# Every fourth half of the latents' weights gets its low part from a ScalarE negative and an adding GpSimd transfer

## The chip, the cores and the metric

The kernel runs on one core of a Trainium2 chip. The metric is the device time of one execution in microseconds, the median of several runs. Before the change it is 989.68 us (three runs, 989.65 to 989.76).

## The reference

One layer of a generator over 256 latent tokens with a prefix of 256 context tokens and a width of 2048. Both streams are normalized, modulated and multiplied by one input projection. A state space group (a scan over chunks of 128 tokens, in both directions) and a gating group share its columns. Only the latents go on to the gates and to the output projection.

```python
hx = _rmsnorm(x, g_pre[l]) * (1.0 + scale[:, None]) + shift[:, None]
zx = hx @ w_in[l]
xh, Bm, Cm, dt, A = _ssd_prep(zx, conv_w[l], conv_b[l], dt_bias[l], a_log[l], ROWS, GRID_W)
y_x, _, _ = _ssd_bidir(xh, Bm, Cm, dt, A, h_f, h_b, True)
...
vn = _rmsnorm(v, g_v).reshape(bsz, L // MLP_CHUNK, MLP_CHUNK, MLP_GROUPS, MLP_GROUP_DIM)
sg = jnp.einsum('gqk,bckgd->bcqgd', w_s, vn) + jnp.swapaxes(b_s, 0, 1)[:, :, None]
y_b = _rmsnorm(u * sg.reshape(bsz, L, MLP_W) * jax.nn.silu(z_mlp), g_mlp)
return jnp.concatenate([y_a, y_b], axis=-1) @ w_out
```

The part at issue is `hx @ w_in` for the columns that only the latents need: four groups of 2048 columns, called v, u, z_mlp and z_ssd.

## The kernel before

Every large product is made of three: weights and activations are each split into a high part, rounded to TensorE's fast float32 form (float32r), and a low part, the rest. The product is high times high, high times low and low times high.

The weights stream in tiles of 128 x 2048 float32 (1 MB). SP issues the loads; a pool of four buffers ("raw") holds them. A tile has two halves of 128 x 1024, numbered u through the whole stream: 0 to 49 are the rest of the first projection, 50 to 177 the latents' (16 blocks of 8 halves), 178 to 241 the output projection. For each half `split` casts the high part on ScalarE (L84) and subtracts it from the weights on VectorE, which gives the low part (L85); the pool "spl" has four buffers for high parts and four for low ones. The first 61 halves are split by another pair of functions (L492 to L502), whose places are written out by hand.

In the latents a half takes twelve matmuls (L1108 to L1110), each with 512 columns: two k-tiles, two groups of 128 tokens, three products. The low part is an operand of L1109. Before the matmuls of half u are issued, `half(u)` has the halves up to u + 3 split:

```python
    def half(u):
        if pos[1]:
            split_to(u + 4)
```

So with four buffers half u + 4 can be cast only when TensorE has read half u for the last time.

In blocks 1 to 8 `gate_tile` puts 16 more loads of 1 MB through the same four raw buffers; VectorE reads each in one pass of 2.29 us (L966, writing "junk"). The work between the blocks (norms, transposes, PSUM evacuations) is put in by a queue with due times. From the latents' second block on, a scheduler sets the order on the engines; each engine then runs its instructions in that order, and so does each queue of DMA issues, SP's and GpSimd's. On GpSimd's queue in this stretch stand ten loads: `cb2`, four of `gvb` (L1035), four of `ws` (L1037), and later `G` (L974).

Of the kernel before, what the change touches and what calls it, by code (L numbers as in the profile page):

```python
# [8 lines left out]
F32 = mybir.dt.float32  # L9
F32R = mybir.dt.float32r  # L10
BF16 = mybir.dt.bfloat16
AF = mybir.ActivationFunctionType
ALU = mybir.AluOpType
PSUM = bass.MemoryType.PSUM

P = 128
# [7 lines left out]
REST = tuple(i for i in range(32) if i not in FIRST)  # L24
# [20 lines left out]
def tile_hybrid_ssd_mlp(  # L45
# [19 lines left out]
    nc = tc.nc  # L65
# [8 lines left out]
    wp = {}  # L74

    def load_raw(src, name):
        raw = wp["raw"].tile([P, 2048], F32, tag="raw", name=name)
        nc.sync.dma_start(raw, src)
        return raw

    def split(raw, n, name):
        hi = wp["spl"].tile([P, n], F32R, tag="hi", name=f"hi_{name}")
        lo = wp["spl"].tile([P, n], F32R, tag="lo", name=f"lo_{name}")
        nc.scalar.copy(hi, raw)  # L84
        nc.vector.tensor_tensor(lo, raw, hi.bitcast(F32), op=ALU.subtract)  # L85
        return hi, lo
# [112 lines left out]
    def ada_load(*cs):  # L199
        for ci in cs:  # L200
            ada_raw[ci] = load_raw(wada[ci], f"ada_{ci}")
# [277 lines left out]
    raws, halves = {}, {}  # L479
    pos = [0, 0]  # L480

    def load_to(n):
        while pos[0] < min(n, len(stream)):
            raws[pos[0]] = load_raw(stream[pos[0]], f"w{pos[0]}")
            pos[0] += 1

    def raw_half(u):
        load_to(u // 2 + 3)
        return raws[u // 2][:, (u % 2) * 1024 : (u % 2 + 1) * 1024]
# [14 lines left out]
    def split_to(n):  # L504
        while pos[1] < min(n, 2 * len(stream)):
            u = pos[1]
            raw = raw_half(u)
            if u in hold:
                for q in range(2):
                    rq, t = raw[:, q * 512 : (q + 1) * 512], hold[u] + q  # L510
                    nc.scalar.copy(hhi[t], rq)
                    nc.vector.tensor_tensor(hlo[t], rq, hhi[t].bitcast(F32), op=ALU.subtract)
            else:
                halves[u] = split(raw, 1024, f"w{u}")
            pos[1] += 1

    def half(u):
        if pos[1]:
            split_to(u + 4)
        else:  # L520
            later(0.1, lambda: split_hi(u + 3))
            later(1.4, lambda: split_lo(u + 3))
        return halves.pop(u)
# [394 lines left out]
    for n, i in enumerate(REST):  # L918
        lat = ORDER[i] >= 24
        ps = acp.tile([P, 256 if lat else 512], F32, tag="acc", name=f"psx{i}")  # L920
        for hf in range(2):
            whi, wlo = half(2 * n + hf)
            for kk in range(8):
                k = 8 * hf + kk
                w = slice(kk * P, (kk + 1) * P)
# [38 lines left out]
    def gate_tile(j):  # L964
        raw = load_raw(wada[2 * KT + j], f"gate{j}")
        nc.vector.scalar_tensor_tensor(L_["junk2"], raw, 1.0, L_["cb2"], op0=ALU.mult, op1=ALU.mult,  # L966
                                       accum_out=gate[:, j : j + 1])
# [121 lines left out]
    for blk in range(16):  # L1089
# [11 lines left out]
        for u in range(8):  # L1101
            whi, wlo = half(base + blk * 8 + u)
            for kk in range(2):
                k = 2 * u + kk
                w = slice(kk * 512, (kk + 1) * 512)
# [223 lines left out]
```

## Time and profile before

| what | value |
|---|---|
| time, median of three runs | 989.68 us (989.65 to 989.76) |
| span of the profiled execution, first to last instruction | 987.9 us |
| the profiled execution's own time | not listed beside its span |
| VectorE busy, from 803 to 941 us | 74.1 of 138 us |
| TensorE busy, from 950 to 988 us | 31.8 of 38 us |
| HBM read over the span | 204.20 MB |

The latents' blocks run from about 440 to 804 us, and the halves that the change touches from 474 to 799 us. A matmul is pipelined: its row shows 0.39 us, but the next one starts 0.23 us later, so the distance of the starts is what it costs. The rows of the profile that follow give an instruction as line, engine, operation, output<-inputs, shapes, count, busy time and mean; the time in brackets is how long the engine had been idle, and what ended that.

### The profile page before, as it was taken

To read this page: it belongs to the slowest core of one execution; us is meant where nothing else is said; L and a number is where in the kernel's file an instruction comes from. 1 tells how busy PE (TensorE), PEld (TensorE's weight loads), DVE (VectorE), ACT (ScalarE), POOL (GpSimd) and SP (SyncE) were. 2 spreads that over 40 slices of the span, in tenths; PEclk is the share of its full clock that TensorE was granted. 3 is DMA by queue.
4 is the path that set the end of the run, shared out by engine and by line. 5 is a ranking of instruction groups with operands and counts; after the bars stand their busy time and mean duration, and the time that the engine had idled before them with its cause. 6 is when DMAs were issued, how large, how long until landed. Compare 5 with 4: busy or idle time off the path is not lost.

```text
span 987.9 us, 13929 instructions
## 1 busy us (share of the span) xinstructions
PE 978.8 (99%) x5502; PEld 792.6 (80%) x5502; DVE 621.4 (63%) x949; ACT 495.4 (50%) x762; POOL 112.5 (11%) x162
## 2 busy tenths in 40 slices
PE   9999999999999999999999999999999999999997
PEld 4688888778887878787888888887888888888885
DVE  4444488868886566756767766767555564445636
ACT  4233358566665554545445343454565563346522
POOL 0000002432453222224000000000000000000000
PEclk9999999999999999999999999999999999999999
DMA  9999844233323424145877768774455446556722
GB/s 372 421 418 418 352 149 166 86 129 128 128 75 139 142 98 145 43 169 206 297 302 284 275 257 296 280 274 170 170 180 203 171 170 213 178 206 228 282 86 85
DMA packets 31985, 207.26 MB, mean 210 GB/s; under 512 B 4128, under 2 KB 4384, under 8 KB 8496
## 3 DMA queue, kind: packets, MB, share of 16 engines
q1 hardware_dynamic: 29232, 192.79, 52.0%
q0 software_dynamic: 2112, 12.65, 3.7%
q8 instruction: 43, 0.70, 0.3%
q10 hardware_dynamic: 576, 0.94, 0.3%
q14 instruction: 22, 0.18, 0.1%
HBM read 204.20 MB, written 2.16 MB: 209 GB/s over the span
## 4 chain that ended last, share of the span: by engine, by line
PE 92%; DMA 4%; ACT 2%; DVE 1%; SPq 0%; issue 0%; ACTq 0%
PE pa L1108 12%; PE pa L1110 12%; PE pa L1109 12%; PE psx L141 9%; PE psx L143 9%; PE psx L142 9%; PE pm L1157 3%; PE pm L1155 3%; PE pm L1156 3%; DMA wst<-in_wst_dram 3%; PE pq L1157 2%; PE pq L1156 2%; PE pq L1155 2%; PE psada L249 2%; PE psc L778 1%; PE pso L831 1%
## 5 line engine op out<-in xcount | busy, mean ns | idle before, releaser
L85 DVE TENSOR_TENSOR lo_w<-w,hi_w 128x1024 fp32r<-128x1024 f32 x173 | 210.7, 1224 | 146.0 <-ACT hi_w L84 145.9
L84 ACT CAST hi_w<-w 128x1024 fp32r<-128x1024 f32 x173 | 182.1, 1053 | 204.5 <-PE pa L1110 129.4
L1108 PE MATMUL pa<-hi_w,hhi 128*128 128x512 f32 x512 | 202.3, 395 | 0.0
L1110 PE MATMUL pa<-hi_w,hlo 128*128 128x512 f32 x512 | 199.5, 390 | 0.0
L1109 PE MATMUL pa<-lo_w,hhi 128*128 128x512 f32 x512 | 199.3, 389 | 0.0
L141 PE MATMUL psx<-hhi,hi_w 128*128 128x512 f32 (+1 forms) x400 | 153.4, 383 | 0.0
L143 PE MATMUL psx<-hhi,lo_w 128*128 128x512 f32 (+1 forms) x400 | 145.9, 365 | 0.0
L142 PE MATMUL psx<-hlo,hi_w 128*128 128x512 f32 (+1 forms) x400 | 145.7, 364 | 0.0
L1108 PEld LDWEIGHTS pa<-hi_w,hhi 128*128 128x128 f32 x512 | 96.2, 188 | 20.5 <-issue 1.6
L1110 PEld LDWEIGHTS pa<-hi_w,hlo 128*128 128x128 f32 x512 | 96.1, 188 | 20.3
L1109 PEld LDWEIGHTS pa<-lo_w,hhi 128*128 128x128 f32 x512 | 96.2, 188 | 19.5 <-issue 0.2
L576 DVE SCALAR_TENSOR_TENSOR xbc<-psx,pc,xbc 128x248 f32<-128x248 f32 (+1 forms) x204 | 83.6, 473 | 34.8 <-ACT xbc L560 33.9
L501 DVE TENSOR_TENSOR lo_w<-w,hi_w 128x1024 fp32r<-128x1024 f32 x61 | 77.1, 1271 | 23.7 <-ACT hi_w L495 23.6
L141 PEld LDWEIGHTS psx<-hhi,hi_w 128*128 128x128 f32 x400 | 75.5, 189 | 13.4 <-issue 2.9
L143 PEld LDWEIGHTS psx<-hhi,lo_w 128*128 128x128 f32 x400 | 75.4, 188 | 12.5
L142 PEld LDWEIGHTS psx<-hlo,hi_w 128*128 128x128 f32 x400 | 75.6, 189 | 12.2 <-issue 1.7
L495 ACT CAST hi_w<-w 128x1024 fp32r<-128x1024 f32 x61 | 63.5, 1044 | 26.0 <-PE psx L142 12.9
L966 DVE SCALAR_TENSOR_TENSOR junk<-gate,cb 128x2048 bf16<-128x2048 f32 x16 | 36.7, 2291 | 24.1 <-DMA gate<-in_wada_dram 24.1
L1155 PE MATMUL pm<-hi_w,hhi 128*128 128x512 f32 x128 | 50.0, 390 | 0.0
L1156 PE MATMUL pm<-lo_w,hhi 128*128 128x512 f32 x128 | 49.9, 390 | 0.0
L1157 PE MATMUL pm<-hi_w,hlo 128*128 128x512 f32 x128 | 49.7, 389 | 0.0
L730 ACT ACTIVATE R<-R,y 128x128 f32<-128x128 f32 x128 | 38.8, 391 | 0.0
(248 smaller groups left out, 1333.6 us busy)
## 6 DMA issues: line engine op xcount, KB each, us to landing
w<-in_wlat_dram SPq DMA_DIRECT2D x64, 1024.0 KB, 4.8
w<-in_wout_dram SPq DMA_DIRECT2D x32, 1024.0 KB, 4.8
ada<-in_wada_dram SPq DMA_DIRECT2D x30, 1024.0 KB, 13.4
w<-in_wxbc_dram SPq DMA_DIRECT2D x25, 1024.0 KB, 4.8
gate<-in_wada_dram SPq DMA_DIRECT2D x16, 1024.0 KB, 5.5
R<-acs POOLq DMA_DIRECT2D x8, 1024.0 KB, 5.2
wst<-in_wst_dram SPq DMA_DIRECT2D x15, 480.0 KB, 14.0
xT<-in_xch_dram SPq DMA_DIRECT2D x4, 1024.0 KB, 8.0
```

The lines of the kernel that those rows point to most:

```text
L84: nc.scalar.copy(hi, raw)
L85: nc.vector.tensor_tensor(lo, raw, hi.bitcast(F32), op=ALU.subtract)
L141: nc.tensor.matmul(ps, lhsT=whi, rhs=hhi[k][:, s], start=start, stop=False)
L142: nc.tensor.matmul(ps, lhsT=whi, rhs=hlo[k][:, s], start=False, stop=False)
L143: nc.tensor.matmul(ps, lhsT=wlo, rhs=hhi[k][:, s], start=False, stop=stop)
L576: nc.vector.scalar_tensor_tensor(ao, zi, cw[:, k : k + 1], ao, op0=ALU.mult, op1=ALU.add)
L1108: nc.tensor.matmul(pa[tk], lhsT=hhi[k][:, t], rhs=whi[:, w], start=k == 0, stop=False)
L1109: nc.tensor.matmul(pa[tk], lhsT=hhi[k][:, t], rhs=wlo[:, w], start=False, stop=False)
L1110: nc.tensor.matmul(pa[tk], lhsT=hlo[k][:, t], rhs=whi[:, w], start=False, stop=k == KT - 1)
L1155: nc.tensor.matmul(p, lhsT=yh[:, t], rhs=whi[:, w], start=j == 0, stop=False)
L1156: nc.tensor.matmul(p, lhsT=yh[:, t], rhs=wlo[:, w], start=False, stop=False)
L1157: nc.tensor.matmul(p, lhsT=yl[:, t], rhs=whi[:, w], start=False, stop=hf == 0 and j == 15)
```

## The change

A second way to split is added, and every fourth half of the latents uses it. The high part is cast as before. ScalarE then writes its negative into the buffer of the low part, and a transfer issued by GpSimd adds the weights to it, from SBUF to SBUF. VectorE has no part in it.

```diff
+    def split_dma(raw, n, name):
+        hi = wp["spl"].tile([P, n], F32R, tag="hi", name=f"hi_{name}")
+        lo = wp["spl"].tile([P, n], F32R, tag="lo", name=f"lo_{name}")
+        nc.scalar.copy(hi, raw)
+        nc.scalar.mul(lo, hi.bitcast(F32), -1.0)
+        nc.gpsimd.dma_start(lo, raw, accum_op=ALU.add)
+        return hi, lo
...
-                halves[u] = split(raw, 1024, f"w{u}")
+                halves[u] = (split_dma if u < 2 * len(REST) + 128 and u % 4 == 3 else split)(raw, 1024, f"w{u}")
```

`len(REST)` is 25, so the halves are those under 178 with u % 4 == 3 that come through this function: 63, 67, ... 175, 29 of them. Lines behind the new function move by 8: L84, L85, L966 and L1035 of before are L92, L93, L974 and L1043 of the change, and its own lines are L84 to L86.

TensorE's order is the same row for row. On the other engines the places below show what moved. In a name like lo_w67_4530 the 67 is the half, in w33_4436 the 33 is the tile.

ScalarE, around half 67 (in the latents' third block), before and then with the change:

```order
L84 CAST hi_w66_4509<-w33_4436 128x1024
L84 CAST hi_w67_4528<-w33_4436 128x1024
L84 CAST hi_w68_4546<-w34_4473 128x1024
L1026 COPY vt_4407<-pa10_4412 128x512
L1028 ACTIVATE sqv10_4575,ssq_4178<-pa10_4412 128x512
```

```order
L92 CAST hi_w66_4510<-w33_4436 128x1024
L84 CAST hi_w67_4529<-w33_4436 128x1024
L85 ACTIVATE lo_w67_4530<-hi_w67_4529 128x1024
L92 CAST hi_w68_4548<-w34_4474 128x1024
L1034 COPY vt_4407<-pa10_4412 128x512
L1036 ACTIVATE sqv10_4577,ssq_4178<-pa10_4412 128x512
```

The negative, L85, stands right behind its cast and ahead of the next cast.

VectorE, the same halves and the first two gate products behind them, before and then with the change:

```order
L85 TENSOR_TENSOR lo_w66_4510<-w33_4436,hi_w66_4509 128x1024
L85 TENSOR_TENSOR lo_w67_4529<-w33_4436,hi_w67_4528 128x1024
L966 SCALAR_TENSOR_TENSOR junk2_4409,gate_114<-gate1_4525,cb2_4408 128x2048
L85 TENSOR_TENSOR lo_w68_4547<-w34_4473,hi_w68_4546 128x1024
L85 TENSOR_TENSOR lo_w69_4565<-w34_4473,hi_w69_4564 128x1024
```

```order
L93 TENSOR_TENSOR lo_w66_4511<-w33_4436,hi_w66_4510 128x1024
L93 TENSOR_TENSOR lo_w68_4549<-w34_4474,hi_w68_4548 128x1024
L974 SCALAR_TENSOR_TENSOR junk2_4409,gate_114<-gate1_4526,cb2_4408 128x2048
L93 TENSOR_TENSOR lo_w69_4567<-w34_4474,hi_w69_4566 128x1024
L93 TENSOR_TENSOR lo_w70_4591<-w35_4508,hi_w70_4590 128x1024
```

The subtract of half 67 is gone, and the gate product now stands behind half 68's subtract instead of ahead of it.

GpSimd's queue, from the third load of `gvb` on, before and then with the change:

```order
L1035 DMA gvb2_5228<-in_gv_dram 128x512
L1035 DMA gvb3_5400<-in_gv_dram 128x512
L1037 DMA ws2_5230<-in_wsp_dram 128x512
L1037 DMA ws3_5402<-in_wsp_dram 128x512
L974 DMA G_5914<-in_gpost_dram 128x2048
```

```order
L86 DMA lo_w83_4834<-w41_4740 128x1024
L1043 DMA gvb2_5238<-in_gv_dram 128x512
L86 DMA lo_w87_4924<-w43_4812 128x1024
L1043 DMA gvb3_5412<-in_gv_dram 128x512
L1045 DMA ws2_5240<-in_wsp_dram 128x512
L86 DMA lo_w91_5006<-w45_4896 128x1024
L86 DMA lo_w95_5098<-w47_4984 128x1024
L1045 DMA ws3_5414<-in_wsp_dram 128x512
```

New transfers stand between and behind the older loads; the load of `G` stands between those of halves 123 and 127.

SP's queue, the loads from the second gate tile on, before and then with the change; in brackets the counters that each waits for (DMAHW and DMASW are landings of transfers from SP's and GpSimd's queues, DVE is VectorE):

```order
L78 DMA gate1_4525<-in_wada_dram 128x2048 [waits DMAHW4_49,DVE_49]
L78 DMA w36_4544<-in_wlat_dram 128x2048 [waits DMAHW5_49,DVE_49]
L78 DMA w37_4586<-in_wlat_dram 128x2048 [waits DMAHW1_49,DVE_49]
L78 DMA gate2_4604<-in_wada_dram 128x2048 [waits DMAHW7_49,DVE_49]
L78 DMA w38_4623<-in_wlat_dram 128x2048 [waits DMAHW0_49,DVE_49]
```

```order
L78 DMA gate1_4526<-in_wada_dram 128x2048 [waits DMAHW4_49,DVE_49]
L78 DMA w36_4546<-in_wlat_dram 128x2048 [waits DMASW7_49,DMAHW5_49,DVE_49,Activation_49]
L78 DMA w37_4588<-in_wlat_dram 128x2048 [waits DMAHW1_49,DVE_49]
L78 DMA gate2_4606<-in_wada_dram 128x2048 [waits DMAHW7_49,DVE_49]
L78 DMA w38_4626<-in_wlat_dram 128x2048 [waits DMASW0_49,DMAHW0_49,DVE_49,Activation_49]
```

The order of the loads is the same. Every second tile goes into the buffer of an odd tile, and there it now waits for the landing of that tile's adding transfer too.

## Prediction

> **What bounds the kernel now.** I read the page's busy times first, then the windows over the stretch that the change touches, then who TensorE waits for, then the order of time inside that stretch. The windows run from where the latents' second block begins to the end of the gate work, and on to the end of the latents; the columns are total width, then busy time (instructions) of each engine, granted clock, DMA share, GB/s.
>
> ```profile
> PE 978.8 (99%) x5502; PEld 792.6 (80%) x5502; DVE 621.4 (63%) x949; ACT 495.4 (50%) x762; POOL 112.5 (11%) x162
> ...
> 460.00:655.00 195.00, 195.00 (x898) 162.61 (x897) 135.13 (x154) 93.37 (x116) 4.41 (x9) 1.00 0.79 293
> 655.00:803.00 148.00, 148.00 (x670) 120.62 (x669) 86.50 (x102) 80.98 (x116) 0.00 (x0) 1.00 0.50 179
> ...
> PE px L1249 <- ACT dg L1248: 1.5, 1, 1.5
> ```
>
> TensorE is busy in every microsecond of both windows at the full granted clock, and the last row is the whole answer to "what does PE wait for" from 400 us on: one wait, at the very end. So VectorE, whose work the change lightens, holds nothing up here: it is at 69% in the first window and 58% in the second. Whatever is saved on it is worth nothing unless TensorE had waited, and that excludes a gain in this stretch. The question is only whether the new transfer makes TensorE wait.
>
> **The deadline of a low part.** A half is split three halves before it is used, and both pools hold four. So its cast starts when TensorE ends the half four back:
>
> ```profile
> 705.32 0.39 PE L1108 MATMUL pa<-hi_w,hhi 128*128 128x512 f32 x1
> 705.54 0.39 PE L1109 MATMUL pa<-lo_w,hhi 128*128 128x512 f32 x1
> ...
> 705.56 1.05 ACT L84 CAST hi_w<-w 128x1024 fp32r<-128x1024 f32 x1 [1.66 <-PE pa L1110]
> 708.29 1.05 ACT L84 CAST hi_w<-w 128x1024 fp32r<-128x1024 f32 x1 [1.68 <-PE pa L1110]
> 711.00 1.05 ACT L84 CAST hi_w<-w 128x1024 fp32r<-128x1024 f32 x1 [1.66 <-PE pa L1110]
> ...
> 706.64 1.23 DVE L85 TENSOR_TENSOR lo_w<-w,hi_w 128x1024 fp32r<-128x1024 f32 x1 [1.49 <-ACT hi_w L84]
> ```
>
> Casts come 2.72 us apart: that is one half's twelve matmuls. The half cast at 705.56 is first multiplied three halves after the one that began at 705.32, and its low part is wanted 0.22 us later (L1109 behind L1108): 705.32 + 3 x 2.72 + 0.22 = 713.70, so 8.14 us after the cast began. VectorE is done at 707.87, 5.8 us early. With the change the chain is cast 1.05, then the negative on ScalarE, also a 128x1024 pass of 1.05, then the hand-overs, some 0.1 in all (VectorE starts 0.03 after the cast's end), then the transfer. That leaves 8.14 - 2.20 = **5.9 us** from issue to landing. A transfer that takes longer stalls TensorE by the excess. No stall is made up: u % 4 == 3 always meets the same buffer of four, and the next cast into it starts only when TensorE has finished the late half, so every split half pays afresh.
>
> **The parts that cost nothing.** Of the halves with u % 4 == 3 in the latents, 51, 55 and 59 are still split by the other path; 63 to 175 remain, **29**. VectorE loses 29 subtracts, ScalarE gains 29 passes:
>
> ```profile
> L85 DVE TENSOR_TENSOR lo_w<-w,hi_w 128x1024 fp32r<-128x1024 f32 x173 | 210.7, 1224 | 146.0 <-ACT hi_w L84 145.9
> L84 ACT CAST hi_w<-w 128x1024 fp32r<-128x1024 f32 x173 | 182.1, 1053 | 204.5 <-PE pa L1110 129.4 <-PE pm L1157 46.5 <-PE pq L1157 19.1
> ```
>
> 29 x 1.224 = 35.5 us off VectorE, worth 0 by the first rows. 29 x 1.053 = 30.5 us onto ScalarE, which idles 204.5 us before its casts alone. Behind the negative stands the next cast, which cannot start for 2.72 us anyway, while cast and negative take 2.1: hidden. PSUM evacuations move by at most that 1.05 us, and the next block writes other banks. At half 151 one PSUM copy stands between cast and negative; it can cost that half about a microsecond. GpSimd was busy 4.41 us and then 0.00 in the two windows, so 29 issues of the 0.54 us below fit. Without this cover ScalarE's 30.5 us would be the price.
>
> On GpSimd's queue six older loads stand among the new transfers, and a transfer waits behind them:
>
> ```profile
> 533.59 0.54 POOL L1035 DMA_DIRECT2D gvb<-in_gv_dram  x1 [71.85 <-DVE vt L1040]
> 539.40 0.54 POOL L1035 DMA_DIRECT2D gvb<-in_gv_dram  x1 [5.28 <-DVE vt L1040]
> 539.93 0.54 POOL L1037 DMA_DIRECT2D ws<-in_wsp_dram  x1
> 562.84 0.54 POOL L1037 DMA_DIRECT2D ws<-in_wsp_dram  x1 [22.37 <-PE psg L1050]
> 643.88 0.54 POOL L974 DMA_DIRECT2D G<-in_gpost_dram  x1 [80.51 <-ACT hi_w L84]
> ```
>
> The casts of the halves right behind them, 87, 91, 99 and 127 by a count of the matmuls:
>
> ```profile
> 531.85 1.05 ACT L84 CAST hi_w<-w 128x1024 fp32r<-128x1024 f32 x1 [0.20 <-PE pa L1110]
> ...
> 544.48 1.05 ACT L84 CAST hi_w<-w 128x1024 fp32r<-128x1024 f32 x1 [1.67 <-PE pa L1110]
> ...
> 568.04 1.05 ACT L84 CAST hi_w<-w 128x1024 fp32r<-128x1024 f32 x1 [1.67 <-PE pa L1110]
> ...
> 648.25 1.05 ACT L84 CAST hi_w<-w 128x1024 fp32r<-128x1024 f32 x1
> ```
>
> Their transfers would be issued 2.2 us later, at 534.1, 546.7, 570.2 and 650.5; the loads in front had been issued at 533.6, 539.9, 562.8 and 643.9. I cost this at 0; a load that came later would hold the transfer by as much.
>
> On SP's queue the load into the buffer of a split odd tile now waits for the transfer's landing, about 2.2 + 6.8 = 9.0 us after the cast, where the subtract freed it 2.3 us after. It lands 4.8 to 5.5 us later (rows below), 13.8 to 14.5 after that cast; its first cast is due five halves on, at 13.6, and VectorE's low part there has 5.8 us to spare. Hidden, with the gate load behind it as the doubtful one (rivals).
>
> **The price of the transfer.** No transfer in the trace goes from SBUF to SBUF or adds, so it is bounded by the others that GpSimd issues.
>
> ```profile
> q1 hardware_dynamic: 29232, 192.79, 52.0%
> q0 software_dynamic: 2112, 12.65, 3.7%
> ...
> w<-in_wlat_dram SPq DMA_DIRECT2D x64, 1024.0 KB, 4.8
> ...
> gate<-in_wada_dram SPq DMA_DIRECT2D x16, 1024.0 KB, 5.5
> R<-acs POOLq DMA_DIRECT2D x8, 1024.0 KB, 5.2
> ...
> gvb<-in_gv_dram POOLq DMA_DIRECT2D x4, 256.0 KB, 6.4
> ws<-in_wsp_dram POOLq DMA_DIRECT2D x4, 256.0 KB, 6.9
> G<-in_gpost_dram POOLq DMA_DIRECT2D x1, 1024.0 KB, 7.4
> ...
> DMA to landing us min/median/max: 4.7/6.4/6.9
> ```
>
> The last row is gvb's. The seven loads R to G are what counts. In quieter surroundings 1 MB takes 5.2 us (R). In the first window, at DMA share 0.79, 256 KB take 4.7 to 6.9 with a median of 6.4, and 1 MB takes 7.4 (G). q0's 3.7% of sixteen engines over 987.9 us for 12.65 MB make 46 engine-us per MB, 2.9 us per MB on sixteen. The new transfer writes 512 KB, but an add has to read both its source and its target: 1 MB read. With R's fixed 5.2 - 2.9 = 2.3 us I take 2.3 + 2.9 = **5.2 us** in quiet and, between gvb's 6.4 and G's 7.4 and nearer the former as it writes half of G, **6.8 us** in the first window. Low end: gvb's 4.7, no stall anywhere. High end: the engines add at half that pace again, 2.3 + 5.8 = 8.1 in quiet and 9.7 in the first window.
>
> [...]
>
> **The sum.** Halves 63 to 123 fall in the first window: 16 of them. Four (87, 95, 103, 111) have extra TensorE work between cast and use:
>
> ```profile
> L1050 PE MATMUL psg<-vt,ws 128*128 128x128 f32 x64 | 7.8, 275 | 0.0
> ```
>
> That is 7.8 us in four blocks, 1.9 each; a busy time counts the pipeline's overlap with the matmul behind it, so I take 1.7, and their deadline is 7.6, above 6.8. The other 12 pay 6.8 - 5.9 = 0.9 us: 10.8 us. The 13 halves of the second window, where DMA share is 0.50, get 5.2 against 5.9: 0. All else 0. The span goes from 987.9 to 998.7; the profiled execution's own time beyond its span is not listed, and the three runs' median of 989.68 lies 1.8 us above it, so I forecast 989.7 + 10.8 = **1000.5 us**. This case's own range is 992 to 1015 (0.2 to 2.1 us for each of the 12).
>
> **Rivals.** (1) *The transfer is hidden everywhere; not slower.* Place: each of the 29. It decides at a landing under 5.9 us. For it: the odd tile's next load now waits for the landing, so the transfer holds off one of the loads that would crowd it, and R and gvb's quickest are under 5.9. Against: the DMA answers of the two windows, whose queue rows stand next; in the first, q1's loads already take 71.7% of the sixteen engines. Price 0: 989.7.
>
> ```profile
> q1 hardware_dynamic: 6991, 50.85, 71.7%
> ...
> q1 hardware_dynamic: 3618, 26.35, 50.6%
> ...
> DVE junk L966 <- DMA gate<-in_wada_dram: 24.1, 11, 5.0
> ...
> L1015 PE MATMUL ptm<-ident,vt 128*128 128x128 f32 x32 | 4.8, 272 | 0.0
> ```
>
> (2) *The add is slow.* At 8.1 and 9.7 us: first window 12 x 3.8 + 4 x 2.1 = 54, second 13 x 2.2 = 29, less 6 x 0.9 = 5 where transposes lengthen the deadline of every other half (4.8 us in four blocks, L1015 above, less overlap): 78, so 1067. Against: nothing in the trace; for: nothing either. (3) *The gate load becomes the wait.* It stands behind the delayed tile load on SP's queue, and VectorE already waits for it eleven times, up to 5.0 us (row above), with the subtracts of three halves queued behind it. Each lateness beyond the 5.8 us to spare reaches TensorE. If the delayed load pushes it by 2 us at eleven places: 22 us, 1012. Against: the gate product now stands one half later on VectorE's queue, which gives 2.7 us back. (4) *Faster.* The tail could start with a shifted ScalarE order; I see no wait there that 2 us could come from.
>
> **Chances.** Forecast 0.42, (1) 0.27, (2) 0.13, (3) 0.15, (4) 0.03. A measurement of this kernel tells 0.2%, 2 us, from no change. Within it is (1): 0.27; faster 0.03; slower 0.70. The range starts at 988.8, below (1), and ends at 1045, which takes in (3) and a rate half way to (2), and leaves out (2)'s full price and (4).
>
> **What would show it.** In the changed trace: TensorE waits on the new transfers in about 12 places of the first window, 0.9 us each, none in the second; the landing of lo_w is about 6.8 and 5.2 us; ScalarE's negative takes 1.05. If lo_w lands under 5.9 everywhere, (1) holds. If the second window shows waits too, the add is slower than two reads (2). If TensorE waits at halves whose low part VectorE makes, it is (3). Any gain would make the argument of the first rows wrong.

## The result and the profile after

| kernel | median us | runs | ratio to before, 95% interval |
|---|---|---|---|
| before | 989.72 | 989.65 to 989.96 (4) | |
| with the change | 1029.42 | 1025.88 to 1030.66 (4) | 1.0391 (1.0379 to 1.0404) |

The change costs 39.7 us. (Of the ten executions of the first kernel under "Where" below, one took 5628 us; its ratio leaves that one out.) The profiled execution took 1030.17 us with a span of 1028.5, which is 40.6 more than the span before. From the page of the changed kernel: busy times, the groups that answer to those of before, and the DMA issues with their median landing.

```profile
PE 993.5 (97%) x5502; PEld 799.7 (78%) x5502; DVE 587.2 (57%) x920; ACT 524.8 (51%) x791; POOL 137.8 (13%) x191
...
L1117 PE MATMUL pa<-lo_w,hhi 128*128 128x512 f32 x512 | 205.6, 402 | 25.9 <-DMA lo_w<-w 25.8
...
L86 POOL DMA_DIRECT2D lo_w<-w x29 | 25.2, 868 | 319.4 <-ACT lo_w L85 319.3
L974 DVE SCALAR_TENSOR_TENSOR junk<-gate,cb 128x2048 bf16<-128x2048 f32 x16 | 36.6, 2291 | 38.5 <-DMA gate<-in_wada_dram 38.5
...
w<-in_wlat_dram SPq DMA_DIRECT2D x64, 1024.0 KB, 5.5
...
gate<-in_wada_dram SPq DMA_DIRECT2D x16, 1024.0 KB, 9.3
lo_w<-w POOLq DMA_DIRECT2D x29, 512.0 KB, 5.3
```

Two numbers make up the loss. TensorE waits 25.8 us at L1117, the first matmul that reads a low part, and it waits there for the new transfer. And it is busy 993.5 us in place of 978.8 with the same 5502 matmuls: 14.7 us more. Together 40.5 of 40.6. The same windows as before show in which stretch (width, busy time of PE, PEld, DVE, ACT and POOL with instructions, granted clock, DMA share, GB/s):

```profile
460.00:655.00 195.00, 176.04 (x766) 143.17 (x765) 98.48 (x117) 91.80 (x107) 16.20 (x22) 0.96 0.83 275
655.00:803.00 148.00, 141.06 (x615) 113.80 (x614) 70.56 (x88) 87.77 (x120) 10.91 (x13) 0.97 0.74 238
```

And what TensorE waits for, the first row of that view (total, times, longest):

```profile
PE pa L1117 <- DMA lo_w<-w: 25.8, 10, 4.2
```

The clock, 1.00 in both windows before, is now 0.96 and 0.97: that is where the longer matmuls come from. The waits are at halves 71, 75, 79, 87, 91, 99, 103, 107, 119 and 127. Behind 127 no half waits.

**One late transfer, followed through.** Half 107: SP's queue, GpSimd's queue and TensorE in the trace after (start, duration, and in brackets the wait in front).

```profile
611.39 0.80 SPq L78 DMA_DIRECT2D w<-in_wlat_dram  x2
612.34 0.33 SPq L78 DMA_DIRECT2D gate<-in_wada_dram  x1
...
616.62 0.86 POOL L86 DMA_DIRECT2D lo_w<-w  x1 [13.30 <-ACT lo_w L85]
...
626.10 0.79 PE L1117 MATMUL pa<-lo_w,hhi 128*128 128x512 f32 x1 [3.63 <-DMA lo_w<-w]
```

Three loads, 3 MB, go out within a microsecond; 4.3 us after the last of them the transfer is issued. What moved on the DMA engines from then on, in two windows, 616.60 to 620.90 and 620.90 to 625.80 (packets, MB, share of sixteen engines):

```profile
q1 hardware_dynamic: 188, 1.41, 100.7%
...
q0 software_dynamic: 144, 0.52, 54.0%
q1 hardware_dynamic: 33, 0.14, 9.0%
```

In the first only the loads (q1): every engine is busy and not one packet of the transfer moves for 4.3 us. All 144 of its packets are in the second, when the loads are nearly done. The landing takes 9.4 us, where 5.9 would have been in time. Compare a transfer behind the gate work, issued at 702.54 us, in the windows 702.50 to 703.95 and 703.95 to 706.65:

```profile
DMA packets 0, 0.00 MB, mean 0 GB/s; under 512 B 0, under 2 KB 0, under 8 KB 0
...
q0 software_dynamic: 144, 0.52, 98.0%
```

Nothing else moves; the first packet comes 1.44 us after the issue, the data take 2.64, and the landing is at 4.4. Behind the wait of half 107 the clock is halved:

```profile
625.01:631.83 6.82, 5.73 (x14) 4.47 (x15) 5.64 (x12) 0.57 (x1) 0.00 (x0) 0.50 0.66 253
631.83:640.00 8.17, 8.17 (x45) 7.04 (x44) 4.57 (x4) 3.63 (x4) 0.86 (x1) 1.00 0.79 247
```

Fourteen matmuls in 6.82 us at clock 0.50, then 45 in 8.17 at 1.00; the row of the first shows 0.79 us (626.10 above) where one at full clock shows 0.39. There are six such stretches in the latents, 3.41 or 6.83 us long, 27.3 us together. TensorE was busy for 24.3 of them, and half of that, 12.1, is most of the 14.7. Of the rest some 1.6 us (an estimate) is overlap lost in front of the ten waits: the last matmul shows its whole 0.39 us there, as no other starts 0.23 us behind it.

### The profile page after: what moved, and what is told of

Its sections match the earlier page's. It is cut to its first block, busy times and chain, and to the rows that moved or that the text cites. A ratio compares the mean times of both kernels' runs of the same rounds, so it can differ in the third digit from the quotient of the medians.

```text
span 1028.5 us, 14053 instructions
## 1 busy us (share of the span) xinstructions
PE 993.5 (97%) x5502; PEld 799.7 (78%) x5502; DVE 587.2 (57%) x920; ACT 524.8 (51%) x791; POOL 137.8 (13%) x191
## 3 DMA queue, kind: packets, MB, share of 16 engines
q0 software_dynamic: 6288, 27.86, 11.1%
## 5 line engine op out<-in xcount | busy, mean ns | idle before, releaser
L93 DVE TENSOR_TENSOR lo_w<-w,hi_w 128x1024 fp32r<-128x1024 f32 x144 | 175.6, 1223 | 186.9 <-ACT hi_w L92 186.8
L1117 PE MATMUL pa<-lo_w,hhi 128*128 128x512 f32 x512 | 205.6, 402 | 25.9 <-DMA lo_w<-w 25.8
L92 ACT CAST hi_w<-w 128x1024 fp32r<-128x1024 f32 x144 | 151.5, 1052 | 143.2 <-PE pa L1118 72.8
L1116 PE MATMUL pa<-hi_w,hhi 128*128 128x512 f32 x512 | 206.6, 404 | 0.0
L1118 PE MATMUL pa<-hi_w,hlo 128*128 128x512 f32 x512 | 204.1, 399 | 0.0
L1117 PEld LDWEIGHTS pa<-lo_w,hhi 128*128 128x128 f32 x512 | 99.1, 194 | 50.7 <-DMA lo_w<-w 30.5
L1116 PEld LDWEIGHTS pa<-hi_w,hhi 128*128 128x128 f32 x512 | 98.8, 193 | 22.0 <-issue 1.6
L1118 PEld LDWEIGHTS pa<-hi_w,hlo 128*128 128x128 f32 x512 | 98.9, 193 | 20.8
L509 DVE TENSOR_TENSOR lo_w<-w,hi_w 128x1024 fp32r<-128x1024 f32 x61 | 77.1, 1270 | 23.7 <-ACT hi_w L503 23.6
L84 ACT CAST hi_w<-w 128x1024 fp32r<-128x1024 f32 x29 | 30.4, 1048 | 80.2 <-PE pa L1118 80.1
L86 POOL DMA_DIRECT2D lo_w<-w x29 | 25.2, 868 | 319.4 <-ACT lo_w L85 319.3
L974 DVE SCALAR_TENSOR_TENSOR junk<-gate,cb 128x2048 bf16<-128x2048 f32 x16 | 36.6, 2291 | 38.5 <-DMA gate<-in_wada_dram 38.5
```

The source lines that it names most:

```text
L509: nc.vector.tensor_tensor(lo, raw_half(u), hi.bitcast(F32), op=ALU.subtract)
L1116: nc.tensor.matmul(pa[tk], lhsT=hhi[k][:, t], rhs=whi[:, w], start=k == 0, stop=False)
L1117: nc.tensor.matmul(pa[tk], lhsT=hhi[k][:, t], rhs=wlo[:, w], start=False, stop=False)
L1118: nc.tensor.matmul(pa[tk], lhsT=hlo[k][:, t], rhs=whi[:, w], start=False, stop=k == KT - 1)
```

## The experiments

Theory at the start: in the gate stretch a transfer waits behind a burst of tile and gate loads, and long waits halve the clock. Rivals: the add is too slow anywhere; ScalarE's negative costs; the gate pass is late on VectorE; GpSimd's queue holds transfers up.

**Where: one part of the halves at a time.**

```diff
-                halves[u] = (split_dma if u < 2 * len(REST) + 128 and u % 4 == 3 else split)(raw, 1024, f"w{u}")
# first kernel
+                halves[u] = (split_dma if 128 <= u < 2 * len(REST) + 128 and u % 4 == 3 else split)(raw, 1024, f"w{u}")
# second kernel
+                halves[u] = (split_dma if u < 128 and u % 4 == 3 else split)(raw, 1024, f"w{u}")
```

> Only the twelve halves from 131 to 175, those behind the gate work, are split with the transfer; the seventeen before them keep VectorE's subtract. Theory (the time is lost only where the gate loads run beside the transfers): TensorE waits at none of the twelve, the clock stays at 1.00, the time is that of before, 989.7, give or take 0.5. Rival (each transfer, with its two reads of SBUF, or each negative on ScalarE costs its share wherever it stands): 12 of 29 parts of the 39.7 us, so about 1006.

> The other side of the run before: only the seventeen halves 63 to 127 are split with the transfer. Theory: all of the loss is here, so 1029.4 within its own scatter of some 3 us, with waits of about 26 us at the first matmul of a low part and half-clock stretches of about 27 us. Rival (every transfer pays): 17 of 29 parts, about 1013.

The first took 990.48 us (ratio 1.0003, 0.9993 to 1.0013), its landings 4.4 to 6.0 us, no wait for a transfer. The second took 1028.88 (1.0389, 1.0373 to 1.0404), 23.5 us of waits in ten places and 27.3 us at half clock. All of the loss lies in the seventeen halves up to 127; the add as such, 4.5 us in the median, is fast enough.

**Who: the negative without the transfer.**

```diff
-        nc.gpsimd.dma_start(lo, raw, accum_op=ALU.add)
+        nc.vector.tensor_tensor(lo, raw, lo.bitcast(F32), op=ALU.add)
```

> ScalarE writes the negative as in the change, at all 29 halves, but VectorE adds the weights to it in place of the transfer: two passes and no GpSimd transfer. Theory: ScalarE's 29 passes of 1.06 us are hidden, VectorE's add ends as early as its subtract did but for 1.06 us, so 989.7, give or take 0.5. Rival (the negative on ScalarE, which delays casts and PSUM copies behind it, makes a part of the loss): up to 29 x 1.06 = 31 us, so anything up to 1020.

990.32 us (1.0005, 0.9995 to 1.0014). ScalarE's passes are free.

**An eighth of the gate loads' bytes: a miss.**

```diff
-        raw = load_raw(wada[2 * KT + j], f"gate{j}")
+        raw = wp["raw"].tile([P, 2048], F32, tag="raw", name=f"gate{j}")[:, 0:256]
+        nc.sync.dma_start(raw, wada[2 * KT + j][:, 0:256])
...
```

> The changed kernel, but each of the sixteen gate loads brings only the first 256 of its 2048 columns (128 KB in place of 1 MB) and VectorE's gate pass reads only these; the gates are therefore not those of the reference. Buffers, queues and the order of the loads are unchanged. Theory (crowding: a transfer waits behind a burst of two tile loads and a gate load, 3 MB): the burst is a third shorter, the transfers' median landing in the gate stretch falls from 7.3 to about 5, most waits go, and what is left is the wait behind G at half 127 with its slow clock, 7.7 us: 997, between 990 and 1003. Rival (the two tile loads alone, held back by the transfer that reads the odd tile, are enough to make it late): over 1015. Rival (gate pass late on VectorE): the waits go too, but the landings stay at 7.3.

1028.88 us (1.0384, 1.0353 to 1.0414): nothing gained, though 14 of 16 MB are gone, and far above the theory's 990 to 1003. TensorE's waits:

```profile
PE pa L1118 <- DMA lo_w<-w: 22.7, 9, 4.6
```

Half 83 on GpSimd's and SP's queues (the second row holds two issues; the other comes 9 us later):

```profile
532.99 0.86 POOL L86 DMA_DIRECT2D lo_w<-w  x1 [13.16 <-ACT lo_w L85]
...
533.38 9.21 SPq L78 DMA_DIRECT2D w<-in_wlat_dram  x2
```

And the one row of a queue in the DMA answer for 532.95 to 537.45:

```profile
q1 hardware_dynamic: 84, 0.69, 70.2%
```

No packet of the transfer moves in it. Here nothing was in flight when the transfer was issued. A single tile load issued 0.4 us *later* had its first packets first (0.96 us after its issue, where the transfer takes 1.44), and the transfer stood for 4.5 us. Six halves of this run have a load issued 0.14 to 0.50 us behind the transfer, and their first packets come after 3.4 to 5.3 us; six have it 0.69 to 1.81 us behind, and theirs come after 1.43 to 1.47. The small gate load lets its buffer go sooner, and the next tile load falls on the transfer instead of ahead of it. So the bytes of the gate loads are not the cause; what counts is whether packets of some load are in flight, or just ahead, when the transfer's first ones are due.

**No gate load at all, then the same loads put elsewhere.** First kernel: VectorE's gate pass reads a tile already in SBUF, and the third load is gone. Second: the kernel with only the late transfers gets a third load there. Third: the same loads without transfers.

```diff
# first kernel
-        raw = load_raw(wada[2 * KT + j], f"gate{j}")
...
-                gate_tile((blk - 1) * 2 + u // 4)
+                gate_tile((blk - 1) * 2 + u // 4, raws[(base + blk * 8 + u + 3) // 2])
# second and third
+            if blk >= 10 and u % 4 == 1:
+                xt = load_raw(wada[2 * KT + (blk - 10) * 2 + u // 4], f"xt{blk}{u}")
+                nc.vector.tensor_scalar(xt, xt, 1.0, 0.0, op0=ALU.mult, op1=ALU.add)
```

> The changed kernel with no gate load at all: VectorE's gate pass, unchanged in length and place, reads the latents' tile that is in SBUF at that moment, and no buffer is taken for it; the gates are therefore not those of the reference. Theory, as it stands after the run with an eighth of the gate loads (it is not their bytes: three loads instead of two in each four halves share four buffers, so that one of them comes free, and is issued, within a microsecond of the transfer's issue, and its packets hold all 16 DMA engines before the transfer's first packet): without the third load the loads fall as they do behind the gate work, both right behind the transfer's landing, and no transfer is late but those at the loads of gv, ws and G: between 990 and 1000. Rival (the stretch is crowded for another reason: PSUM work, the loads of gv and ws, GpSimd's passes): over 1010.

> The positive side: the kernel that splits only the halves 131 to 175 with the transfer (990.5), to which twelve loads of 1 MB are added, one in each four halves, at the same place and from the same buffers as the gate loads before them, each with a VectorE pass over it in place. Nothing else changes. Theory: the third load brings the collision to the late transfers: landings of 6 to 10 us in place of 4.5, waits at up to all twelve, some with slow clock: 1000 to 1025. Rival (the gate stretch has something else that makes transfers late): 990 to 992, landings of 4.5.

> The counterpart of the run with twelve added loads (1007.7): the same twelve loads and VectorE passes behind the gate work, added to the kernel before, with VectorE's subtract at every half and no transfer. Theory (a load costs only where a transfer meets it): 989.7 to 990.5, the clock at 1.00. Rival (the added loads or passes slow the stretch by themselves, and that run showed no meeting): about 1007.

The first: 998.35 us (1.0083, 1.0066 to 1.0100), inside the theory's range. TensorE's one wait for a transfer:

```profile
PE pa L1116 <- DMA lo_w<-w: 6.1, 1, 6.1
```

The transfer that it is for, half 119's, behind G on GpSimd's queue:

```profile
631.52 0.55 POOL L981 DMA_DIRECT2D G<-in_gpost_dram  x1 [11.98 <-DVE gk L992]
632.10 0.86 POOL L86 DMA_DIRECT2D lo_w<-w  x1
```

And the landings of all 29, from the view of the low part's tile:

```profile
DMA to landing us min/median/max: 4.4/4.4/9.5
```

With the wait come 6.83 us at half clock, in which TensorE was busy for 3.12, so 1.6 us more; together 7.7 of the 9.1 us by which the span is above that of before. The other sixteen transfers of the stretch are on time. VectorE's gate passes are all still there, so they are not what made the transfers late. The second kernel: 1007.66 us (2 runs; 1.0178, 1.0158 to 1.0199), inside the theory's range, where the one without the added loads had 990.48. Four transfers that had no wait now have one:

```profile
PE pa L1117 <- DMA lo_w<-w: 8.3, 4, 2.9
```

Three of them, 7.7 us together, stand behind three loads each, their first packets at 2.9 to 4.3 us. The fourth, half 139's 0.5 us, is of another kind: nothing was in flight, but GpSimd's issue itself took 1.84 us in place of 0.87, beside the added pass of VectorE (1.21 us).

```profile
687.12 1.84 POOL L86 DMA_DIRECT2D lo_w<-w  x1 [12.79 <-ACT lo_w L85]
```

The third: 990.41 (1.0003, 0.9994 to 1.0013). So in these kernels it takes both, a third load in each four halves and the transfer.

**The hold taken away, and the transfers thinned out.** The transfer reads the weights' tile and holds it till it lands; only then can SP load into that buffer, which bunches the loads. First kernel: it adds the high part instead. Second: `u % 8 == 7`.

```diff
-        nc.gpsimd.dma_start(lo, raw, accum_op=ALU.add)
+        nc.gpsimd.dma_start(lo, hi.bitcast(F32), accum_op=ALU.add)
```

> The changed kernel, its transfers adding the high part instead of the weights, so the low parts are zero and not those of the reference; the weights' tile is no longer held by the transfer and comes free at ScalarE's cast. Theory 1 (the hold is what bunches three loads into one burst in front of the next transfer): the loads spread as they do before the change, most transfers land in under 5.9, 990 to 1000. Theory 2 (with three loads in each four halves some load always meets the transfer; unheld, the load into the odd tile is issued about 1 us before the transfer and takes the engines first): first packets still come at 2.5 to 4.5, 1010 to 1040.

> The change at every eighth half instead of every fourth: 63, 71, ... 175, fifteen transfers, nine of them in the gate stretch, two neighbours 21.8 us apart. Theory 1 (a transfer is late because the one before it held a tile and so set off a burst 5 us ahead of it): each transfer's burst is over long before the next, first packets at 1.5 to 2.5, landings under 5.9, also at G, which no late transfer holds back: 990 to 995. Theory 2 (each transfer beside the gate loads is late by itself): nine waits of 1.5 to 4 with slow clock behind the longer ones, 1005 to 1020.

The first: 1079.45 us (1.0898, 1.0876 to 1.0919), twice the loss and above the ranges of both theories. SP's and GpSimd's queues at a half behind the gate work:

```profile
730.06 0.33 SPq L78 DMA_DIRECT2D w<-in_wlat_dram  x1
...
731.42 0.86 POOL L86 DMA_DIRECT2D lo_w<-hi_w  x1 [13.63 <-ACT lo_w L85]
```

The DMA answers for 731.40 to 734.10 and 734.10 to 737.60:

```profile
q1 hardware_dynamic: 107, 0.88, 91.4%
...
q0 software_dynamic: 144, 0.52, 75.6%
q1 hardware_dynamic: 30, 0.11, 8.8%
```

TensorE's waits:

```profile
PE pa L1117 <- DMA lo_w<-hi_w: 60.8, 22, 4.5
```

Now ScalarE's cast frees the odd tile, and its load is issued 1.36 us ahead of nearly every transfer. One load costs 1.3 us there (first packet at 2.75), and two of them, 1.36 and 0.94 us ahead in most of the gate stretch, mostly put it at 4.9 to 5.2. Theory 2's account held, with a price that it had too low: the hold does not make transfers late, it only decides which loads meet them, and in the change it keeps one out of the way. The second kernel: 1002.97 (1.0131, 1.0114 to 1.0147), between the two theories and nearer theory 2. Transfers 22 us apart are late too; SP's and GpSimd's queues at half 95:

```profile
558.76 0.33 SPq L78 DMA_DIRECT2D w<-in_wlat_dram  x1
559.89 0.33 SPq L78 DMA_DIRECT2D gate<-in_wada_dram  x1
...
561.88 0.90 POOL L86 DMA_DIRECT2D lo_w<-w  x1 [17.95 <-ACT lo_w L85]
```

TensorE's waits:

```profile
PE pa L1117 <- DMA lo_w<-w: 9.1, 6, 3.4
```

Two loads 3.1 and 2.0 us ahead of it are enough: its first packet came at 4.45. Six of nine wait here, 1.5 us in the mean, against 2.6 for the ten of seventeen in the change. That is mostly a matter of deadlines: three of the six (95, 103, 111) have the longer one, and the six land 6.3 to 9.3 us after their issue, the ten 7.3 to 11.0. Whether one transfer's landing makes the next one later is not shown by this.

**The same transfer without the add.**

```diff
-        nc.gpsimd.dma_start(lo, raw, accum_op=ALU.add)
+        nc.gpsimd.dma_start(lo, raw)
```

> The changed kernel, its transfers without the adding: the same 29 issues copy the weights into the low part's buffer (512 KB read once, not two reads), so the low parts are not those of the reference. Theory: the copy's data pass in about 1.3 us in place of 2.6, a quiet landing is 3.1, and a transfer held back by three loads lands at 6 to 7.5 in place of 8.5 to 9.5: waits under 1.7 us, no slow clock but at G: 992 to 1005. Rival (the first packet's delay by the loads is all that counts): 1020 or more. Rival (the adding alone makes transfers late): 990.

1015.76 us (1.0269, 1.0251 to 1.0287), above the theory's range and below the rival's. In quiet the plain copy's data take 1.40 us where the add's take 2.64, a ratio of 1.9, and it lands at 2.8; that part was right. But the first packet still came as late as 4.9 us. TensorE's waits, then the landings:

```profile
PE pa L1117 <- DMA lo_w<-w: 16.3, 10, 3.8
```

```profile
DMA to landing us min/median/max: 2.8/5.4/8.8
```

So 26 of the 40 us are left without any adding: the waiting for the first packet weighs more than the add. (The loads fall a little differently here, so the other 14 us are not the add's price alone.)

**G on GpSimd's queue.** Half 127's transfer stands behind the 1 MB load of G, which landed only 11.1 us after its issue, where it took 7.4 before (trace after):

```profile
678.75 0.55 POOL L982 DMA_DIRECT2D G<-in_gpost_dram  x1 [4.85 <-DMA lo_w<-w]
683.94 0.86 POOL L86 DMA_DIRECT2D lo_w<-w  x1 [4.64 <-ACT lo_w L85]
```

```diff
-                halves[u] = (split_dma if u < 2 * len(REST) + 128 and u % 4 == 3 else split)(raw, 1024, f"w{u}")
+                halves[u] = (split_dma if u < 2 * len(REST) + 128 and u % 4 == 3 and u != 127 else split)(raw, 1024, f"w{u}")
```

> The changed kernel but for half 127, which VectorE splits: its transfer stands behind the 1 MB load of G on GpSimd's queue and landed 11 us after its issue. Theory: the wait of 4.3 us at 127 and the 6.8 us at half clock behind it (3.4 us) go: 1029.4 - 7.7 = 1021.7. Rival (G collides with the next transfer instead, or the loads shift so that another half pays): 1026 or more.

1024.62 us (1.0352, 1.0336 to 1.0367): 4.8 less, between the two. The wait at 127 went, but 24.9 us of waits in ten other places were left: which halves are late shifts from kernel to kernel.

**The slow clock by itself.** No transfer; VectorE repeats its subtract at six halves.

```diff
                 halves[u] = split(raw, 1024, f"w{u}")
+                for _ in range({131: 6, 139: 7, 147: 8, 155: 6, 163: 7, 171: 8}.get(u, 0)):
+                    nc.vector.tensor_tensor(halves[u][1], raw, halves[u][0].bitcast(F32), op=ALU.subtract)
```

> The kernel before, without any transfer; at six halves behind the gate work VectorE writes the low part 6, 7 or 8 times more, with the same numbers (131: 6, 139: 7, 147: 8, 155: 6, 163: 7, 171: 8). At 1.22 us each and 5.8 us of margin TensorE should wait 1.5, 2.7 and 4.0 us, twice each: 16.4 us in all. Theory (a wait of about 3 us or more is followed by 3.4 or 6.8 us at half clock, each 3.4 of them worth 1.7 us; a wait of 1.7 or less is not): one or more such stretches behind each of the two longest waits, none behind the shortest: 989.7 + 16.4 + 3.4 to 7 = 1009.5 to 1013. Rival (the slow clock comes from the transfers or from the DMA traffic, not from the wait): clock 1.00 throughout, 1006.

1032.86 us (2 runs; 1.0433, 1.0412 to 1.0454). The waits are longer than set, 28.1 us in place of 16.4, since VectorE's products for the transposes (L1077) stood behind the repeats. TensorE's waits:

```profile
PE pa L1111 <- DVE lo_w L516: 10.4, 5, 4.0
PE ptm L1017 <- DVE vt L1077: 9.2, 6, 2.8
PE pta L1017 <- DVE y L1077: 8.5, 5, 3.0
```

The first of them on TensorE's timeline:

```profile
669.98 0.33 PE L1017 MATMUL ptm<-ident,vt 128*128 128x128 f32 x1 [1.50 <-DVE vt L1077]
...
700.35 0.44 PE L1017 MATMUL ptm<-ident,vt 128*128 128x128 f32 x2 [2.82 <-DVE vt L1077]
702.08 1.33 PE L1017 MATMUL ptm<-ident,vt 128*128 128x128 f32 x5 [1.30 <-DVE vt L1077]
```

And windows behind the first of these waits, and over and behind the next two:

```profile
671.80:675.30 3.50, 3.24 (x17) 2.58 (x18) 3.50 (x6) 2.18 (x6) 0.00 (x0) 1.00 0.53 159
698.16:701.57 3.41, 0.44 (x2) 0.20 (x2) 3.41 (x5) 0.72 (x2) 0.00 (x0) 1.00 0.57 171
701.57:704.98 3.41, 2.90 (x10) 2.61 (x11) 3.41 (x5) 1.92 (x5) 0.00 (x0) 0.50 0.55 178
704.98:708.40 3.42, 3.42 (x16) 2.81 (x16) 1.60 (x4) 1.66 (x3) 0.00 (x0) 1.00 0.63 266
```

The wait of 1.5 us leaves the clock alone; the waits of 2.8 and 1.3 halve it for 3.41 us. Half clock follows a long wait without any transfer: the theory's side, though the time was 20 us above its range.

## Why the prediction was wrong

Slower was forecast, +10.8 us, and it is +39.7. The steps:

- *TensorE bounds, VectorE's saving is worth nothing.* Right: VectorE lost 34.2 us of work, and the time rose.
- *ScalarE's 30.5 us are hidden.* Right: 990.32 with the negative alone.
- *5.9 us from issue to landing, and no stall is made up.* Right: landing less wait is 5.8 us at six of the ten waits (half 107: 9.44 - 3.63), and the waits and the longer busy time add up to 40.5 of the span's 40.6. The longer deadline of 87, 95, 103 and 111, 7.6 us, is right too: 87 and 103 landed after 9.13 and 8.80 us and waited 1.53 and 1.19, which leaves 7.6 both times. 95 and 111 landed after 5.3 and 4.7.
- *5.2 us in quiet, so nothing in the second window.* Right: 4.5 in the median where only these halves were split so, and no wait at the twelve from 131 on; 127 is the case of G below. The transfer's data, put at 2.9 us for 1 MB read, took 2.64 in quiet; the rows count 0.52 MB and do not show the reads.
- *6.8 us in the first window.* **This step failed.** It took the landing for one figure of a crowded stretch, read from loads of gv and G. The transfer has no such figure: its data take 2.64 us and its first packet 1.44 when nothing is in flight, and up to 4.5 us when tile or gate loads are. The mean was close, and that was no help: the sixteen transfers from 63 to 123 land after 7.1 us in the mean, but between 4.4 and 9.6, and only what lies over the deadline counts. Nine of them waited 21.6 us together, where 6.8 for each gave 10.8. The buffers fix when the loads are issued relative to the transfer. The prediction followed them as far as the loads' own lateness; what they do to a transfer only rival 1 asked, and with the other sign. With G's, ten waits of 2.6 us in the mean came in place of twelve of 0.9: +15.0 us.
- *Nothing else.* **This failed too:** the sum had no term for the clock. The busy time grew by 14.7 us, the other half of the miss, 12.1 of it at half clock, and the run with VectorE's repeats shows that waits alone do it.
- *The transfers behind older loads on GpSimd's queue, at 0.* Wrong for G: the wait at 127 was 4.2 us, and splitting it on VectorE brings 4.8; the text had named the condition, a load that comes later. G was issued 5.2 us ahead of the transfer, about as expected (6.6), but it took 11.1 us to land, 3.7 more than before, and the text had asked only when G is issued.

Of the rivals, the hidden transfer holds behind the gate work alone. The slow add falls: the add lands after 4.4 us in quiet where that rival had 8.1, and 26 us of loss stay without it. The gate load as a wait falls as well: VectorE waits for it 38.5 us instead of 24.1, but no wait of TensorE of 0.3 us or more is for a low part that VectorE makes.

What stays open is why the transfer's packets stand while loads are in flight. GpSimd's issue took 0.86 us at half 107 and 0.87 in quiet, so its row does not tell the two apart; what holds the packets was not tried. Once the transfer has begun, both queues' packets do mix: at half 111 of the run with an eighth of the gate loads, 144 packets of the transfer and 136 of a load passed in the same 5.6 us. From 1.44 us after the issue, when a transfer in quiet has its first packet, 128 of the profile's load packets went ahead at half 107; no run here shows what sets that number.

## What to carry to other kernels

Price a small transfer inside a stream of large loads by the phase at which it meets them, not by the mean load of the stretch: find what frees each load's buffer, and lay the loads' time (here 4.6 to 8.3 us from issue to landing, between 460 and 803 us of the kernel before) beside the transfer's issue. Ask then what its own landing frees. And where TensorE was never idle before, add the slow clock behind the longer waits: in the change all six waits of 2.7 us and more were followed by it, the four of 1.5 us and less were not, and it cost about half as much again as the waits.

## What the runs showed of the hardware

- The transfer's first packet came 1.43 to 1.50 us after its issue in quiet (1.10 for the plain copy). It came at 2.7 behind one load issued 1.36 us earlier (the run that adds the high part), 4.3 behind three issued 5.2 to 4.3 earlier (half 107 of the change), 4.5 with one issued 0.4 *later* (half 83 with an eighth of the gate loads). Two issued 5.5 and 5.0 earlier left it at 1.45 (half 159 of the change), and loads issued 0.69 to 1.81 later at 1.43 to 1.47 (six halves with an eighth of the gate loads).
- In ten runs in which TensorE waited, between 460 and 900 us, the changes of the clock fall on a grid of 3.41 us: 48 windows of the grid at full clock were followed by half clock, and TensorE was busy for at most 0.44 of each; 1181 were followed by full clock, and it was busy for at least 0.45. Back to full went 48 half-clock windows, busy 0.85 or more; 12 stayed at half clock, 0.82 or less.
- GpSimd's issue of the transfer took 0.86 to 0.92 us in the change. Once, in the run with the added late loads, beside VectorE's added pass over 128x2048 f32 (1.21 us), it took 1.84, and the first packet came at 2.42 with nothing in flight; why is not shown.
